# A two-layer hybrid encoder on one core: the left operands of the MLP's seven products are ordered behind the last bank read of the block before, squares go to ScalarE, derived low parts are made in two instructions

## The chip, the core and the metric

The kernel runs on one core of a Trainium2 chip. The metric is the device time of one execution in microseconds (us); lower is better. Times of before come from three plain runs and from one profiled execution, whose trace is what is read here.

## What is computed

The reference is a two-layer encoder trunk on 512 frames of width 1024 in float32. Layer 0 mixes tokens with a sparse attention, layer 1 with a latent attention, and each layer ends in a dense MLP with a squared ReLU. The change touches the two MLPs only:

```python
D_MODEL = 1024
SEQ = 512
DEPTH = 2
D_FF = 4 * D_MODEL

def squared_relu_mlp(h, w_up, w_down):
    a = jax.nn.relu(h @ w_up)
    return (a * a) @ w_down

    for i in range(DEPTH):
        h = rms_norm(x, attn_norm[i])
        ...
        h = rms_norm(x, mlp_norm[i])
        x = x + squared_relu_mlp(h, mlp_w_up[i], mlp_w_down[i])
    return rms_norm(x, final_norm)
```

## The kernel before, in words

**Three passes for one product.** Every float32 operand is split into a high part (rounded to the format that TensorE multiplies, `fp32r`) and a low part (what is left), and a product is three matmuls: high by high, high by low, low by high. For weights `Weights.convert` (from L112) does this: ScalarE casts the raw tile to `w_hi` (L143), GpSimd subtracts to get `w_lo` (L144), one instruction each for a tile of 128x1024. For activations in the MLP `part` (L1098 to L1104) does it on ScalarE (`lh`, L1102) and VectorE (`ll`, L1103), 128x512 each.

**The MLP in blocks.** `mlp` cuts the 4096 hidden columns into NB = 8 blocks of FB = 512. `up(b)` makes the hidden block `u`: four groups of 24 matmuls (8 slices of the width, three passes), 96 in all, each group into one PSUM bank; `square` then writes relu squared to `u` with a Relu on ScalarE (L1073) and a multiply on VectorE (L1074, which reads the bank again). For blocks 0 to 6 the second product is made by `left` and `down_quarters`: with `u` cut in two by two pieces and the block's weights too, seven products of half size replace eight (Winograd's form). `left` makes the seven left operands from the four pieces: four additions or subtractions on VectorE (L1114, L1115, L1117, L1119), in place in `u`, and seven `part`s. `Weights.quarters` makes the seven right operands from four quarter tiles `quad`: four subtractions on VectorE (L86), in place too, each followed by the conversion of its result. Because they are in place, a later subtraction waits until GpSimd has read the value before: the chain is `quad` subtraction, cast, low part, next subtraction. The seven weights of a block are called Q1 to Q7 below, the four weight tiles of its up half U1 to U4.

**Down.** `down_quarters` does seven steps of 12 matmuls, 84 in all. A step writes two PSUM banks, `pa` in the odd steps and `pb` in the even ones, and after its first six and its last six matmuls VectorE adds the bank to the residual `x` (L1141): 14 bank reads a block. Most steps go on accumulating in a bank that was read two steps earlier, so step s+2 waits for the bank reads of step s. The last block goes through `down`, which makes the full product.

**What sets the order.** The program is traced in the order `left(u of block b-1)`, `up(b)`, `down_quarters` of block b-1, and a scheduler with a timeline of its own orders the instructions of every engine at compile time. Each engine then runs its queue strictly in that order. `W.take` hands out converted weights; `WBUFS` = 5 pairs of `w_hi` and `w_lo` exist, so a tile is converted when TensorE has finished with the one five before it.

Of the kernel before, what the change touches and what calls it, by code (L numbers as in the profile page):

```python
# [11 lines left out]
F32 = mybir.dt.float32  # L12
F32R = mybir.dt.float32r
I32 = mybir.dt.int32
AF = mybir.ActivationFunctionType
OP = mybir.AluOpType
# [37 lines left out]
class Weights:  # L54
# [57 lines left out]
    def convert(self):  # L112
        i = len(self.done)
        if i >= len(self.items):
            return
        while len(self.raw) <= i:
            self.fetch()
        nc = self.nc
        src, a, n, engs, heads = self.items[i]
        raw = self.raw[i]  # L120
        if callable(src):
            heads = None
            if callable(raw):
                raw = raw()
        hi = self.parts.tile([P, a * n], F32R, name=f"w{i}_hi", tag="whi")
        lo = self.parts.tile([P, a * n], F32R, name=f"w{i}_lo", tag="wlo")
        views = [(raw, hi, lo)]
        if heads is not None:

            views = []  # L130
            for s in range(2):
                v = raw.rearrange("p (k h s d) -> p k h s d", k=a, h=heads, s=2)[:, :, :, s, :]
                o = [t.rearrange("p (k s h d) -> p k s h d", k=a, s=2, h=heads)[:, :, s, :, :] for t in (hi, lo)]
                views.append((v, *o))
        for v, h, l in views:
            if engs[0] == "p":
                shape = list(v.shape)
                one = self.ones
                while len(one.shape) < len(shape):
                    one = one[:, None]  # L140
                nc.gpsimd.tensor_tensor(h, v, one.to_broadcast(shape), op=OP.mult)
            else:
                nc.scalar.copy(h, v)  # L143
            (nc.gpsimd if engs[1] == "p" else nc.vector).tensor_sub(l, v, h.bitcast(F32))  # L144
        r = lambda t: t.rearrange("p (a n) -> p a n", a=a)
        self.done.append((r(hi), r(lo)))
        while len(self.raw) < min(len(self.done) + RAWS, len(self.items)):
            self.fetch()
# [50 lines left out]
def trunk(ctx: ExitStack, tc: tile.TileContext, x, positions, attn_norm, mlp_norm, a_w_in, a_w_out,  # L199
          b_w_in, b_q_norm, b_kv_norm, b_w_q_up, b_w_kv_up, b_w_out, mlp_w_up, mlp_w_down,  # L200
          final_norm, out):
    nc = tc.nc
# [6 lines left out]
    def bank(name, i):  # L209
        return psum.tile([P, 512], F32, name=name, tag=f"bank{i}")  # L210
# [9 lines left out]
    def mm3(ps, lh, ll, rh, rl, first, last):  # L220
        nc.tensor.matmul(ps, lh, rh, start=first, stop=False)  # L221
        nc.tensor.matmul(ps, lh, rl, start=False, stop=False)  # L222
        nc.tensor.matmul(ps, ll, rh, start=False, stop=last)  # L223
# [835 lines left out]
    def mlp(i, nm, follower):  # L1059
        with ExitStack() as sm:  # L1060
            mp = sm.enter_context(tc.tile_pool(name=f"mlp{i}", bufs=1, reuse_waits="tile"))
            W.quads = mp
            hi, lo = nm.hi, nm.lo
            up_b, dn_b = Banks(0, 1, 4, 5), Banks(6, 7, 2, 3)

            def up_mm(ps, ws, f, t0, t1):
                for k in range(KD):
                    wh, wl = ws[k // 4]
                    mm3(ps[:, t0:t1], wh[:, k % 4, f * P:(f + 1) * P], wl[:, k % 4, f * P:(f + 1) * P],
                        hi[:, k, t0:t1], lo[:, k, t0:t1], k == 0, k == KD - 1)  # L1070

            def square(ps, u, f):
                nc.scalar.activation(u[:, f, :], ps, AF.Relu)  # L1073
                nc.vector.scalar_tensor_tensor(u[:, f, :], ps, 0.0, u[:, f, :], op0=OP.max, op1=OP.mult)  # L1074

            def up(b):
                u = mp.tile([P, 4, S], F32, name="u", tag="u", bufs=2)
                if b == 0:

                    ws = W.take(2) + W.take(2, 2)  # L1080
                    pp = [up_b("up") for _ in range(4)]
                    for f in range(4):
                        up_mm(pp[f], ws[f // 2 * 2:][:2], f % 2, 0, S // 2)
                        if f % 2:
                            nm.turn(NT - 2 + f // 2)
                    for f in range(4):
                        up_mm(pp[f], ws[f // 2 * 2:][:2], f % 2, S // 2, S)
                        square(pp[f], u, f)
                    return u
                for c in range(FB // 256):  # L1090
                    ws = W.take(2)
                    for f in range(2):
                        ps = up_b("up")
                        up_mm(ps, ws, f, 0, S)
                        square(ps, u, 2 * c + f)
                return u

            def part(v):  # L1098

                lh = mp.tile([P, 2, S // 2], F32R, name="lh", tag="lh", bufs=8)  # L1100
                ll = mp.tile([P, 2, S // 2], F32R, name="ll", tag="ll", bufs=8)
                nc.scalar.copy(lh, v)  # L1102
                nc.vector.tensor_sub(ll, v, lh.bitcast(F32))  # L1103
                return lh, ll  # L1104

            def blocks(u):

                return [[u[:, 2 * k:2 * k + 2, i * 256:(i + 1) * 256] for k in range(2)] for i in range(2)]

            def left(u):  # L1110

                (a, b), (c, d) = blocks(u)
                l11, l22 = part(a), part(d)
                nc.vector.tensor_add(d, c, d)  # L1114
                nc.vector.tensor_sub(c, a, c)  # L1115
                s3 = part(c)
                nc.vector.tensor_sub(a, d, a)  # L1117
                s2, s1, l12 = part(a), part(d), part(b)
                nc.vector.tensor_sub(b, b, a)  # L1119
                return [l11, s3, s2, l22, s1, l12, part(b)]  # L1120

            def down_quarters(ops):

                pa, pb = [bank("dn", 6), bank("dn", 7)], [bank("dn", 2), bank("dn", 3)]

                steps = ((pa, True, (0, 0)), (pb, True, (1, 1)), (pa, False, (1, 0)), (pb, False, (1, 0)),
                         (pa, False, (1, 1)), (pb, True, (0, 0)), (pa, False, (0, 1)))  # L1130
                for (lh, ll), (pp, first, (i, j)) in zip(ops, steps):
                    wh, wl = W.take()[0]
                    cs = slice(j * 512, (j + 1) * 512)
                    for t in range(2):
                        ts = slice(t * P, (t + 1) * P)
                        for k in range(2):
                            for m, (l, r) in enumerate(((lh, wh), (lh, wl), (ll, wh))):
                                nc.tensor.matmul(pp[t], l[:, k, ts], r[:, k, :], start=first and k == 0 and m == 0,  # L1138
                                                 stop=k == 1 and m == 2, skip_group_check=True)
                        x = xt[2 * i + t]  # L1140
                        nc.vector.tensor_add(x[:, cs], pp[t], x[:, cs])  # L1141

            def down(u, after):
                ops = [[part(v) for v in row] for row in blocks(u)]
                ws = W.take(FB // P)
                for t in range(NT):
                    ts = slice(t % 2 * P, (t % 2 + 1) * P)
                    for c in range(2):
                        cs = slice(c * 512, (c + 1) * 512)
                        ps = dn_b("dn")  # L1150
                        for k in range(4):
                            wh, wl = ws[k]
                            lh, ll = ops[t // 2][k // 2]
                            mm3(ps, lh[:, k % 2, ts], ll[:, k % 2, ts], wh[:, 0, cs], wl[:, 0, cs], k == 0, k == 3)
                        nc.vector.tensor_add(xt[t][:, cs], ps, xt[t][:, cs])
                        after(t, c)

            prev = up(0)
            for b in range(1, NB):
                ops = left(prev)  # L1160
                prev = up(b)
                down_quarters(ops)
            nxt = follower()
            down(prev, nxt.follow)
        return nxt
# [10 lines left out]

    nm = mixer_a()
    nm = mlp(0, nm, lambda: Norm(attn_norm[1]))
    nm = mixer_b(nm)
    mlp(1, nm, Final)  # L1180


# [22 lines left out]
```

## Time and profile before

| What | us |
|---|---|
| median of three runs | 1190.31 (1190.16 to 1190.56) |
| profiled execution | 1191.61 |
| its span in the trace | 1189.8 |
| TensorE matmul busy | 1124.6 (95%) |
| VectorE busy | 876.9 (74%) |
| GpSimd busy | 650.0 (55%) |
| ScalarE busy | 561.8 (47%) |
| from the first matmul of `down_quarters` to the first of `down` in MLP 0 | 307.10 to 585.55 |
| the same in MLP 1 | 882.83 to 1161.21 |

In the rows of the profile PE is TensorE's matmul side, PEld its weight loads, DVE VectorE, ACT ScalarE, POOL GpSimd, SP SyncE. A row of the timeline has the start in us, the duration in us, engine, line, operation, output and inputs, shape and count, and in brackets how long the engine was idle before it and what ended that. A row of the chain of work that ended last has start, length and the work. A row of the groups has line, engine, operation, names, shapes and count, then busy us and the mean ns of one, then idle us before them and what ended it. Matmul durations are modelled with an overlap; the distance of their starts is the pace.

### The profile page before, as it was taken

How to read it: one execution, taken by the hardware profiler on the slowest of the kernel's cores; microseconds unless marked ns; L12 is line 12 of the kernel's file. 1: busy time of each engine (PE TensorE's matmuls, PEld its weight loads, DVE VectorE, ACT ScalarE, POOL GpSimd, SP SyncE). 2: the span in 40 equal slices, each digit the busy share in tenths (PEclk: the TensorE clock that was granted, in tenths of full speed). 3: DMA queues.
4: the chain of work that ended last, by engine and by line, in shares of the span. 5: the costliest groups of instructions: out<-in, count | busy, mean ns of one | idle time of the engine just before them, and what ended most of it. 6: DMA issues, size and time to landing. Idle time of an engine off the chain costs nothing.

```text
span 1189.8 us, 15782 instructions
## 1 busy us (share of the span) xinstructions
PE 1124.6 (95%) x5721; PEld 947.9 (80%) x5721; DVE 876.9 (74%) x1483; ACT 561.8 (47%) x1051; POOL 650.0 (55%) x397
## 2 busy tenths in 40 slices
PE   6899899999999999999999899899999999999997
PEld 5778778879777787787889788797987787787786
DVE  7599998765958757857567888985587857866864
ACT  5443786644433443433345666563443433434342
POOL 4457432553656755765603642735556665765771
PEclk9899899999999999999999999999999999999999
DMA  6422100251224323322312210111513322322401
GB/s 205 115 63 92 51 1 2 72 175 57 89 64 131 105 73 106 124 72 88 91 51 77 74 54 1 59 49 54 189 57 109 121 74 89 124 89 71 142 18 71
DMA packets 65605, 99.55 MB, mean 84 GB/s; under 512 B 3188, under 2 KB 41848, under 8 KB 65528
## 3 DMA queue, kind: packets, MB, share of 16 engines
q1 hardware_dynamic: 65528, 98.55, 25.8%
q8 instruction: 45, 0.74, 0.2%
q14 instruction: 32, 0.26, 0.1%
HBM read 96.44 MB, written 2.10 MB: 83 GB/s over the span
## 4 chain that ended last, share of the span: by engine, by line
PE 66%; DVE 28%; ACT 2%; issue 2%; DMA 1%; SPq 0%; POOL 0%; DVEq 0%; POOLq 0%; ACTq 0%
PE dn L1138 10%; PE up L223 10%; PE up L222 9%; PE up L221 9%; DVE ll L1103 5%; DVE x L1141 5%; PE s_ps L508 3%; PE o_ps L570 3%; PE wo_ps L221 2%; DVE u L1117 2%; DVE u L1115 2%; PE wo_ps L222 2%; PE wo_ps L223 2%; DVE u L1114 2%; PE pt_ps L527 2%
## 5 line engine op out<-in xcount | busy, mean ns | idle before, releaser
L144 POOL TENSOR_TENSOR w_lo<-w_raw,w_hi 128x1024 fp32r<-128x1024 f32 (+4 forms) x117 | 276.9, 2380 | 153.2 <-ACT w_hi L143 152.9
L144 POOL TENSOR_TENSOR w_lo<-quad,w_hi 128x1024 fp32r<-128x1024 f32 x98 | 247.2, 2541 | 138.6 <-ACT w_hi L143 138.6
L222 PE MATMUL up<-hT_lo,w_hi 128*128 128x512 f32 (+1 forms) x576 | 210.5, 366 | 0.0
L221 PE MATMUL up<-hT_hi,w_hi 128*128 128x512 f32 (+1 forms) x576 | 209.4, 366 | 0.1
L223 PE MATMUL up<-hT_hi,w_lo 128*128 128x512 f32 (+1 forms) x576 | 208.6, 366 | 0.0
L143 ACT CAST w_hi<-quad 128x1024 fp32r<-128x1024 f32 x98 | 101.7, 1051 | 164.1 <-DVE quad L86 135.1
L1138 PE MATMUL dn<-w_hi,lh 128*128 128x512 f32 x392 | 155.6, 397 | 20.9 <-DVE x L1141 20.1
L1141 DVE TENSOR_TENSOR x<-dn,x 128x512 f32<-128x512 f32 x196 | 130.4, 683 | 46.3 <-PE dn L1138 45.4
L1138 PE MATMUL dn<-w_hi,ll 128*128 128x512 f32 x392 | 152.8, 390 | 0.0
L1138 PE MATMUL dn<-w_lo,lh 128*128 128x512 f32 x392 | 152.7, 390 | 0.0
L143 ACT CAST w_hi<-w_raw 128x1024 fp32r<-128x1024 f32 (+6 forms) x108 | 109.1, 1018 | 74.9 <-PE dn L1138 23.3
L1103 DVE TENSOR_TENSOR ll<-u,lh 128x512 fp32r<-128x512 f32 x106 | 130.4, 1243 | 5.0 <-ACT lh L1102 4.8
L1102 ACT CAST lh<-u 128x512 fp32r<-128x512 f32 x106 | 63.8, 618 | 132.9 <-DVE u L1119 62.0
L86 DVE TENSOR_TENSOR quad<-quad 128x1024 f32<-128x1024 f32 x56 | 68.4, 1222 | 73.6 <-POOL w_lo L144 73.6
L222 PEld LDWEIGHTS up<-hT_lo,w_hi 128*128 128x128 f32 x576 | 108.6, 189 | 17.6 <-DVE hT_lo L422 0.2
L223 PEld LDWEIGHTS up<-hT_hi,w_lo 128*128 128x128 f32 x576 | 108.6, 189 | 17.5
L221 PEld LDWEIGHTS up<-hT_hi,w_hi 128*128 128x128 f32 x576 | 108.1, 189 | 17.9 <-ACT hT_hi L421 0.3
L1138 PEld LDWEIGHTS dn<-w_hi,lh 128*128 128x128 f32 x392 | 73.5, 188 | 47.0 <-DVE x L1141 31.9
L521 ACT ACTIVATE p<-p,m 128x128 f32<-128x128 f32 (+3 forms) x128 | 71.9, 563 | 32.4 <-DVE m L516 31.8
L1138 PEld LDWEIGHTS dn<-w_hi,ll 128*128 128x128 f32 x392 | 73.6, 188 | 15.5
L1138 PEld LDWEIGHTS dn<-w_lo,lh 128*128 128x128 f32 x392 | 73.6, 188 | 14.4
L1074 DVE SCALAR_TENSOR_TENSOR u<-up,u 128x512 f32<-128x512 f32 x64 | 44.0, 687 | 55.2 <-ACT u L1073 55.2
(223 smaller groups left out, 2313.1 us busy)
## 6 DMA issues: line engine op xcount, KB each, us to landing
w_raw<-in_mlp_w_up_dram SPq DMA_DIRECT2D x64, 512.0 KB, 3.6
quad<-in_mlp_w_down_dram SPq DMA_DIRECT2D x56, 512.0 KB, 3.6
w_raw<-in_a_w_in_dram SPq DMA_DIRECT2D x12, 512.0 KB, 3.6
w_raw<-in_a_w_out_dram SPq DMA_DIRECT2D x8, 512.0 KB, 3.2
w_raw<-in_mlp_w_down_dram SPq DMA_DIRECT2D x8, 512.0 KB, 3.6
w_raw<-in_b_w_out_dram SPq DMA_DIRECT2D x8, 512.0 KB, 3.7
x<-in_x_dram SPq DMA_DIRECT2D x4, 512.0 KB, 7.4
w_raw<-in_b_w_kv_up_dram SPq DMA_DIRECT2D x4, 512.0 KB, 3.8
```

The source lines that it names most:

```text
L86: self.nc.vector.tensor_sub(q[o], q[l], q[r])
L143: nc.scalar.copy(h, v)
L144: (nc.gpsimd if engs[1] == "p" else nc.vector).tensor_sub(l, v, h.bitcast(F32))
L221: nc.tensor.matmul(ps, lh, rh, start=first, stop=False)
L222: nc.tensor.matmul(ps, lh, rl, start=False, stop=False)
L223: nc.tensor.matmul(ps, ll, rh, start=False, stop=last)
L521: nc.scalar.activation(U["p"][:, :N], U["p"][:, :N], AF.Exp, bias=U["m"], scale=-1.0, accum_out=pair["sums"][:, c:c + 1])
L1074: nc.vector.scalar_tensor_tensor(u[:, f, :], ps, 0.0, u[:, f, :], op0=OP.max, op1=OP.mult)
L1102: nc.scalar.copy(lh, v)
L1103: nc.vector.tensor_sub(ll, v, lh.bitcast(F32))
L1138: nc.tensor.matmul(pp[t], l[:, k, ts], r[:, k, :], start=first and k == 0 and m == 0, stop=k == 1 and m == 2, skip_group_check=True)
L1141: nc.vector.tensor_add(x[:, cs], pp[t], x[:, cs])
```

## The change

Three edits. `down_quarters` returns its last bank read, and from the second block on `left` is traced with `issue_after` that instruction, which puts every VectorE instruction of `left` behind it in VectorE's queue (what `left` does on ScalarE is not bound by it). `square` multiplies on ScalarE, by a Square activation of `u` in place, in place of the VectorE multiply. `convert` makes the low part of a weight that comes from `quarters` (its `src` is a function) in two GpSimd instructions of 512 columns; other weights keep one of 1024.

```diff
-            (nc.gpsimd if engs[1] == "p" else nc.vector).tensor_sub(l, v, h.bitcast(F32))
+            if callable(src):
+
+                for c in range(0, a * n, 512):
+                    cs = slice(c, c + 512)
+                    nc.gpsimd.tensor_sub(l[:, cs], v[:, cs], h[:, cs].bitcast(F32))
+            else:
+                (nc.gpsimd if engs[1] == "p" else nc.vector).tensor_sub(l, v, h.bitcast(F32))
...
                 nc.scalar.activation(u[:, f, :], ps, AF.Relu)
-                nc.vector.scalar_tensor_tensor(u[:, f, :], ps, 0.0, u[:, f, :], op0=OP.max, op1=OP.mult)
+                nc.scalar.activation(u[:, f, :], u[:, f, :], AF.Square)
...
-                        nc.vector.tensor_add(x[:, cs], pp[t], x[:, cs])
+                        last = nc.vector.tensor_add(x[:, cs], pp[t], x[:, cs])
+                return last
...
             prev = up(0)
+            last = None
             for b in range(1, NB):
-                ops = left(prev)
+                with tc.issue_after(last.ins) if last is not None else ExitStack():
+                    ops = left(prev)
                 prev = up(b)
-                down_quarters(ops)
+                last = down_quarters(ops)
```

The changed file has other line numbers: L1141 becomes L1147, L1102 and L1103 become L1108 and L1109, L1114, L1115, L1117 and L1119 become L1120, L1121, L1123 and L1125, L1073 and L1074 become L1079 and L1080 (now on ScalarE), L144 becomes L148 for the two halves. Texts below use the numbers of before.

First place, VectorE in the second block of MLP 0. Before, its queue from the third bank read of a `down_quarters` on, in which `x_85` to `x_88` are the four tiles of the residual:

```order
L1141 TENSOR_TENSOR x_87<-dn,x_87 128x512
L1103 TENSOR_TENSOR ll<-u,lh 128x512
L1141 TENSOR_TENSOR x_88<-dn,x_88 128x512
L1114 TENSOR_TENSOR u<-u 128x2x256
L1141 TENSOR_TENSOR x_87<-dn,x_87 128x512
L1115 TENSOR_TENSOR u<-u 128x2x256
L1141 TENSOR_TENSOR x_88<-dn,x_88 128x512
L1117 TENSOR_TENSOR u<-u 128x2x256
```

Now, from behind the last bank read of a `down_quarters` to the first of the next:

```order
L1109 TENSOR_TENSOR ll<-u,lh 128x512 x2
L1120 TENSOR_TENSOR u<-u 128x2x256
L1121 TENSOR_TENSOR u<-u 128x2x256
L1123 TENSOR_TENSOR u<-u 128x2x256
L86 TENSOR_TENSOR quad<-quad 128x1024
L1109 TENSOR_TENSOR ll<-u,lh 128x512 x2
L86 TENSOR_TENSOR quad<-quad 128x1024
L1109 TENSOR_TENSOR ll<-u,lh 128x512 x2
L1125 TENSOR_TENSOR u<-u 128x2x256
L1109 TENSOR_TENSOR ll<-u,lh 128x512
L86 TENSOR_TENSOR quad<-quad 128x1024 x2
L1147 TENSOR_TENSOR x_85<-dn,x_85 128x512
```

All eleven instructions of `left` and the four `quad` subtractions now stand between two sets of 14 bank reads, and the 14 follow each other with nothing between them.

Second place, ScalarE over the same block. Before, the casts of the four up weights (`w_raw`) alternate with those of the left operands (`lh`):

```order
L143 CAST w_hi<-w_raw 128x1024
L1102 CAST lh<-u 128x512 x3
L143 CAST w_hi<-w_raw 128x1024
L1102 CAST lh<-u 128x512
L143 CAST w_hi<-w_raw 128x1024
L1102 CAST lh<-u 128x512
L143 CAST w_hi<-w_raw 128x1024
L143 CAST w_hi<-quad 128x1024
L1073 ACTIVATE u<-up 128x512
L143 CAST w_hi<-quad 128x1024
L1073 ACTIVATE u<-up 128x512
```

Now:

```order
L143 CAST w_hi<-w_raw 128x1024 x4
L143 CAST w_hi<-quad 128x1024
L1108 CAST lh<-u 128x512 x4
L1079 ACTIVATE u<-up 128x512
L1080 ACTIVATE u<-u 128x512
L143 CAST w_hi<-quad 128x1024
L1079 ACTIVATE u<-up 128x512
L1108 CAST lh<-u 128x512
L1080 ACTIVATE u<-u 128x512
L1108 CAST lh<-u 128x512
L143 CAST w_hi<-quad 128x1024
```

The four up casts and the first `quad` cast now stand ahead of the left operands' casts, and a Square follows each Relu. On GpSimd the order is unchanged, each `w_lo<-quad` row of 1024 columns being two rows of 512; on TensorE three matmuls of the next `up` move by some places within the last steps of `down_quarters`; SyncE's queue is the same.

## The prediction

> **What bounds the kernel now.** I read the page first, for the engines and for the chain that ended last.
>
> ```profile
> span 1189.8 us, 15782 instructions
> PE 1124.6 (95%) x5721; PEld 947.9 (80%) x5721; DVE 876.9 (74%) x1483; ACT 561.8 (47%) x1051; POOL 650.0 (55%) x397
> ...
> PE 66%; DVE 28%; ACT 2%; issue 2%; DMA 1%; SPq 0%; POOL 0%; DVEq 0%; POOLq 0%; ACTq 0%
> ```
>
> TensorE is the bound, but 28% of the chain lies on VectorE, so somewhere TensorE waits for it. Second, the chain in order of time over one middle block of MLP 0.
>
> ```profile
> 437.87 4.09 PE dn L1138 x18
> ...
> 444.04 2.13 DVE u L1114
> 446.17 0.60 DVE x L1141
> 446.77 2.21 DVE u L1115
> ...
> 449.58 2.22 DVE u L1117
> ...
> 454.20 2.75 DVE ll L1103
> 456.95 0.61 DVE x L1141
> ...
> 457.61 3.02 PE dn L1138 x12
> ```
>
> The chain leaves TensorE soon after the seven products begin, runs along VectorE's queue through the subtractions and low parts of `left`, and comes back by a bank read (L1141): the reads are late because `left` stands between them. Third, the timeline of TensorE at that place and at the starts of `dn`, the first matmul of a `down_quarters` (rows of several windows).
>
> ```profile
> 307.10 0.39 PE L1138 MATMUL dn<-w_hi,lh 128*128 128x512 f32 x1
> ...
> 328.81 0.50 PE L1138 MATMUL dn<-w_hi,lh 128*128 128x512 f32 x1 [1.46 <-DVE x L1141]
> ...
> 351.84 0.39 PE L1138 MATMUL dn<-w_hi,lh 128*128 128x512 f32 x1
> ...
> 455.76 0.39 PE L1138 MATMUL dn<-w_hi,ll 128*128 128x512 f32 x1
> 457.61 0.50 PE L1138 MATMUL dn<-w_hi,lh 128*128 128x512 f32 x1 [1.46 <-DVE x L1141]
> ...
> 480.64 0.39 PE L1138 MATMUL dn<-w_hi,lh 128*128 128x512 f32 x1
> ...
> 566.51 0.39 PE L1138 MATMUL dn<-w_hi,lh 128*128 128x512 f32 x1
> ...
> 882.83 0.39 PE L1138 MATMUL dn<-w_hi,lh 128*128 128x512 f32 x1
> ...
> 927.57 0.39 PE L1138 MATMUL dn<-w_hi,lh 128*128 128x512 f32 x1
> ...
> 1142.17 0.39 PE L1138 MATMUL dn<-w_hi,lh 128*128 128x512 f32 x1
> ```
>
> How fast a `down_quarters` can be is shown by the last of MLP 0, for which no `left` is queued between the bank reads (the chain again):
>
> ```profile
> 566.67 19.04 PE dn L1138 x84
> ```
>
> 84 matmuls in 19.04 us are 0.2267 us each. From one start of `dn` to the next there are 84 + 96 = 180 matmuls, 40.80 us at that pace. Measured: 351.84 - 307.10 = 44.74, then (566.51 - 351.84) / 5 = 42.93 in each of five blocks; in MLP 1 44.74 and (1142.17 - 927.57) / 5 = 42.92. So TensorE loses 3.94 + 5 x 2.13 + 3.94 + 5 x 2.12 = 29.1 us in twelve blocks. This is all that the change can win there.
>
> **Why `left` is slow under the products.** The groups by shape:
>
> ```profile
> L144 POOL TENSOR_TENSOR w_lo<-quad,w_hi 128x1024 fp32r<-128x1024 f32 x98 | 247.2, 2541 | 138.6 <-ACT w_hi L143 138.6
> L144 POOL TENSOR_TENSOR w_lo<-w_raw,w_hi 128x512 fp32r<-128x512 f32 x6 | 7.7, 1304 | 0.0
> L1103 DVE TENSOR_TENSOR ll<-u,lh 128x512 fp32r<-128x512 f32 x106 | 130.4, 1243 | 5.0 <-ACT lh L1102 4.8
> L1141 DVE TENSOR_TENSOR x<-dn,x 128x512 f32<-128x512 f32 x196 | 130.4, 683 | 46.3 <-PE dn L1138 45.4
> L86 DVE TENSOR_TENSOR quad<-quad 128x1024 f32<-128x1024 f32 x56 | 68.4, 1222 | 73.6 <-POOL w_lo L144 73.6
> L1074 DVE SCALAR_TENSOR_TENSOR u<-up,u 128x512 f32<-128x512 f32 x64 | 44.0, 687 | 55.2 <-ACT u L1073 55.2
> L1115 DVE TENSOR_TENSOR u<-u 128x512 f32<-128x512 f32 x14 | 28.8, 2059 | 0.0
> L1119 DVE TENSOR_TENSOR u<-u 128x512 f32<-128x512 f32 x14 | 9.7, 690 | 0.4
> L1102 ACT CAST lh<-u 128x512 fp32r<-128x512 f32 x106 | 63.8, 618 | 132.9 <-DVE u L1119 62.0
> L1073 ACT ACTIVATE u<-up 128x512 f32<-128x512 f32 x64 | 37.9, 593 | 38.5 <-PE up L223 38.4
> ```
>
> L1115 and L1119 are the same operation on the same shape, at 2.06 and 0.69 us. What differs is GpSimd beside them:
>
> ```profile
> 448.39 2.86 POOL L144 TENSOR_TENSOR w_lo<-w_raw,w_hi 128x1024 fp32r<-128x1024 f32 x1
> 454.00 5.19 POOL L144 TENSOR_TENSOR w_lo<-w_raw,w_hi 128x1024 fp32r<-128x1024 f32 x2 [2.76 <-ACT w_hi L143]
> ...
> 462.22 2.41 POOL L144 TENSOR_TENSOR w_lo<-w_raw,w_hi 128x1024 fp32r<-128x1024 f32 x1 [3.02 <-ACT w_hi L143]
> ```
>
> L1117 began at 449.58 inside the first of these and ended 451.80, 0.55 after it (448.39 + 2.86 = 451.25); the `ll` at 454.20 ended at 456.95, 0.35 after half of the pair at 454.00. So a VectorE instruction with both inputs in SBUF waits for the GpSimd instruction that has begun, then takes 0.6; the bank reads, with one input in PSUM, take 0.68 whatever GpSimd does. [...]
>
> **The change part by part.**
>
> Order of `left`. It removes from the 14 bank reads everything between them, so each can go at about its bank's end, as in the stretch of 19.04 us. Gain 29.1 us, if nothing else comes late. What it moves: seven `ll`, four subtractions of `left` and four `quad` subtractions now stand in the stretch of the next `up`, 91 matmuls or 20.6 us, ahead of the next bank reads. I set 0 at the end of the last `dn` matmul. The last bank read, 0.68 long, is done at about 1. Two `ll` and L1114 share the time with Q1's low part, whose cast waits for the end of `dn`: L1114 done at about 5.2, L1115 and L1117 at 6.4. First `quad` 6.4 to 7.6, `ll` of the third and fourth operand to 8.8 (their casts ran meanwhile on ScalarE), second `quad` to 10.0. Then the in-place chain, its steps by these rows:
>
> ```profile
> 470.15 1.05 ACT L143 CAST w_hi<-quad 128x1024 fp32r<-128x1024 f32 x1 [4.58 <-DVE quad L86]
> ...
> 471.28 2.40 POOL L144 TENSOR_TENSOR w_lo<-quad,w_hi 128x1024 fp32r<-128x1024 f32 x1 [4.29 <-ACT w_hi L143]
> ...
> 473.71 1.23 DVE L86 TENSOR_TENSOR quad<-quad 128x1024 f32<-128x1024 f32 x1 [1.29 <-POOL w_lo L144]
> ...
> 478.53 1.23 DVE L86 TENSOR_TENSOR quad<-quad 128x1024 f32<-128x1024 f32 x1 [1.29 <-POOL w_lo L144]
> ```
>
> Cast 10.2 to 11.2, Q2's low part in two halves of 1.30 with one `ll` let in between, to 14.6; the rest of `left` is done by then; third `quad` to 16.0; cast to 17.2, Q3's low part to 19.9, fourth `quad` to 21.1. The next `dn` starts at 20.6, and its first six matmuls end at 22.0, so VectorE is free a microsecond early. TensorE would be held only if the first bank read ended after step 3 begins, 20.6 + 24 x 0.2267 = 26.0, that is if the fourth `quad` ended after 25.1: 4 us of room. Weights, at the same pace of one low part per 2.6 and 2.4 us: Q4 ready at about 25 (wanted at step 4, 28.8), Q7 at 32.5 (step 7, 38.1), U1's low part at 35 (its first matmul in the queue, 37.9). Before, the fourth `quad` began at 478.53, 2.1 us ahead of the start of `dn` at 480.64; by this schedule it begins 0.7 ahead, so the chain has moved by 1.4 us of its room.
>
> In the first block of each MLP `left` isn't bound, but the 3.94 us lost there are of the same kind: the wait at 328.81 is for a bank read, behind the `left` of the second block, and that one is bound.
>
> Squares. 64 VectorE multiplies of 0.69 go, four a block; none is on the chain, so their going is worth 0. ScalarE gets 64 squares. No row has this one; the nearest are the Relu at 593 ns and the cast of the same shape from SBUF at 618. I take 0.62, since input and output are in SBUF, 2.5 us a block on an engine that is busy 17.2 of 42.93:
>
> ```profile
> 437.87:480.80 42.93, 41.39 (x181) 33.62 (x181) 30.82 (x33) 17.20 (x24) 27.98 (x11) 1.00 0.31 98
> ```
>
> (The columns are the stretch, its length, and busy us of TensorE, its weight loads, VectorE, ScalarE and GpSimd.) What waits behind them are the second `quad` cast and two casts of `left`, at most 1.2 us of the 4 us room. ScalarE's queue keeps the two table loads that it had. Cost 0, within 1 us either way at the first and last block of an MLP, where `u` is awaited.
>
> Halves. 98 GpSimd instructions become 196. Two of 1.30 are 2.61, against 2.41 undisturbed: +0.2 us each, 1.4 a block on GpSimd, not on the path. They halve what VectorE waits. [...]
>
> Sum: 1191.61 - 29.1 = 1162.5 for a profiled execution. That one stood 1.3 above the median, so 1161.2 for the median.
>
> **The rivals.**
>
> 1. GpSimd's round becomes the bound. By the schedule above the last low part of a round ends at about 41 to 43 with the period at 40.80: Q1 cannot begin early, and Q2, Q3 and Q4 each wait for VectorE. If `left` and GpSimd stop each other more than I count, say by 2 us a block, the round takes 42 to 43, the lateness adds up by 1.5 a block, the 3 to 4 us of room last two or three blocks, and the other three pay 1.5 to 2: 2 x 3 x 1.75 = 10 us lost again, 1172. For it: the round is within 2 us of the period, and low parts do get longer beside VectorE (2.86 at 448.39 against 2.41 at 462.22). [...] Against: today's collisions lengthen GpSimd's 11 instructions only from 26.5 (11 x 2.41) to 27.98, and at a period of 40.80 it would still be idle for 11 us.
>
> 2. Slower: the waits of `left` stay as long as they are under the products. Place: the fourth `quad` and behind it the bank reads. If all eleven instructions of `left` cost 2.06, they are 22.7 us, with the four `quad`s 4.9, and the last ends at 1 + 27.6 = 28.6, 3.5 past the limit of 25.1. TensorE then loses 3.5 a block, against 2.13 now: 10 x 1.4 - 2 x 0.4 = 13 more, 1203. It decides from 27.2 on, 6 us later than I expect. Against: GpSimd is idle for good parts of this stretch (3.02 and 4.29 us ahead of the low parts at 462.22 and 471.28), and the halves cut each wait.
>
> 3. It doesn't do what it says: the loss is elsewhere, and 1190 stays. Against: the chain names the bank reads in the block shown, and the five middle blocks of either MLP have the same mean period to 0.01 us.
>
> **How the numbers follow.** Forecast 0.72, rival 1 0.16, rival 2 0.07, rival 3 0.05. The gain needs no price that the trace lacks, only that about 15 us of VectorE work end within 24. The range goes from 1159 (2 us for the bounds of the squares and of the pace) to 1172, which takes in rival 1 up to its price. A measurement of this kernel can tell 0.2%, 2.4 us, from no change. Faster by more: forecast, rival 1 and a little of rival 3, 0.89; within: 0.04; slower: 0.07.
>
> **What would show it.** Right: starts of `dn` 40.8 apart, no wait of a `dn` matmul for L1141 within a block, the chain almost all on TensorE there, L1115 well under 2.06, a square near 0.62, halves near 1.30. The steps are wrong if the periods lie above 41.3 with waits for weights (rival 1), if the fourth `quad` ends more than 4.5 us after the start of `dn` (rival 2), or if the periods are 40.8 and the time has not fallen, which would mean time lost outside the MLPs.

## The result and the profile after

| Kernel | Median of its runs, us | Ratio to before (95%) |
|---|---|---|
| before | 1190.43 (1190.16 to 1190.56) | |
| changed | 1162.22 (1161.57 to 1163.72) | 0.9765 [0.9748, 0.9782] |
| changed, a second time, beside a before of 1191.59 | 1162.62 | 0.9759 [0.9745, 0.9772] |

The ratios here and below leave out one execution of the kernel with the order alone, which took 1249.79 us at a granted clock of 0.85.

The profiled execution took 1162.26 us, 29.35 less than that of before. First the page: the span, the engines, and the shares of the chain that ended last.

```profile
span 1160.5 us, 15969 instructions
PE 1116.6 (96%) x5721; PEld 949.8 (82%) x5721; DVE 782.3 (67%) x1419; ACT 604.3 (52%) x1115; POOL 666.0 (57%) x495
...
PE 79%; DVE 12%; issue 3%; ACT 3%; POOL 1%; DMA 1%; SPq 0%; DVEq 0%; POOLq 0%; ACTq 0%
```

TensorE's share of the chain rose from 66% to 79%, VectorE's fell from 28% to 12%. The timeline of TensorE at starts of `dn` in the changed kernel:

```profile
306.27 0.39 PE L1144 MATMUL dn<-w_hi,lh 128*128 128x512 f32 x1
...
347.07 0.39 PE L1144 MATMUL dn<-w_hi,lh 128*128 128x512 f32 x1
...
551.07 0.39 PE L1144 MATMUL dn<-w_hi,lh 128*128 128x512 f32 x1
...
868.03 0.39 PE L1144 MATMUL dn<-w_hi,lh 128*128 128x512 f32 x1
...
1112.83 0.39 PE L1144 MATMUL dn<-w_hi,lh 128*128 128x512 f32 x1
```

347.07 - 306.27 = 40.80, (551.07 - 306.27) / 6 = 40.80, (1112.83 - 868.03) / 6 = 40.80. From the first start to the last, MLP 0 takes 244.80 in place of 259.41 and MLP 1 244.80 in place of 259.34: 29.15 of the 29.35 us. The remainder outside these stretches is small because two changes cancel: the first `dn` starts 0.83 us earlier, and MLP 0's last block takes 0.7 us longer. The groups by shape of the changed kernel:

```profile
L148 POOL TENSOR_TENSOR w_lo<-quad,w_hi 128x512 fp32r<-128x512 f32 x196 | 275.0, 1433 | 162.9 <-ACT w_hi L143 160.3 <-PE up L229 2.4
L1147 DVE TENSOR_TENSOR x<-dn,x 128x512 f32<-128x512 f32 x196 | 135.0, 691 | 138.4 <-PE dn L1144 138.4
L1109 DVE TENSOR_TENSOR ll<-u,lh 128x512 fp32r<-128x512 f32 x106 | 99.4, 968 | 40.8 <-ACT lh L1108 40.8
L1080 ACT ACTIVATE u<-u 128x512 f32<-128x512 f32 x64 | 40.4, 632 | 1.7
L1120 DVE TENSOR_TENSOR u<-u 128x512 f32<-128x512 f32 x14 | 23.3, 1664 | 0.5
L1121 DVE TENSOR_TENSOR u<-u 128x512 f32<-128x512 f32 x14 | 12.6, 901 | 0.5
```

L1120 and L1121 (L1114 and L1115 of before) fell from 2003 and 2059 ns to 1664 and 901. The bank read still takes 0.69, but it now waits 138.4 us for `dn` where it waited 46.3: at the bank reads VectorE waits for TensorE, no longer the other way round. A square takes 632 ns, a half 1433.

The timeline between two sets of bank reads in a middle block of MLP 0; the next `dn` starts at 469.47. First VectorE, then GpSimd, then two rows of ScalarE.

```profile
449.04 0.69 DVE L1147 TENSOR_TENSOR x<-dn,x 128x512 f32<-128x512 f32 x1 [0.67 <-PE dn L1144]
449.65 4.28 DVE L1109 TENSOR_TENSOR ll<-u,lh 128x512 fp32r<-128x512 f32 x2
453.97 1.67 DVE L1120 TENSOR_TENSOR u<-u 128x512 f32<-128x512 f32 x1
...
457.00 1.22 DVE L86 TENSOR_TENSOR quad<-quad 128x1024 f32<-128x1024 f32 x1
...
470.34 1.22 DVE L86 TENSOR_TENSOR quad<-quad 128x1024 f32<-128x1024 f32 x1 [3.74 <-POOL w_lo L148]
471.49 0.68 DVE L1147 TENSOR_TENSOR x<-dn,x 128x512 f32<-128x512 f32 x1
```

```profile
449.29 2.40 POOL L150 TENSOR_TENSOR w_lo<-w_raw,w_hi 128x1024 fp32r<-128x1024 f32 x1 [0.47 <-ACT w_hi L143]
451.65 3.44 POOL L148 TENSOR_TENSOR w_lo<-quad,w_hi 128x512 fp32r<-128x512 f32 x2
461.86 3.48 POOL L148 TENSOR_TENSOR w_lo<-quad,w_hi 128x512 fp32r<-128x512 f32 x2 [6.77 <-ACT w_hi L143]
467.77 2.54 POOL L148 TENSOR_TENSOR w_lo<-quad,w_hi 128x512 fp32r<-128x512 f32 x2 [2.42 <-ACT w_hi L143]
```

```profile
448.16 1.05 ACT L143 CAST w_hi<-w_raw 128x1024 fp32r<-128x1024 f32 x1 [4.59 <-DMA w_raw<-in_mlp_w_up_dram]
449.17 1.05 ACT L143 CAST w_hi<-quad 128x1024 fp32r<-128x1024 f32 x1
```

The schedule of the prediction is there, in its order, but 1.6 to 1.8 us later from the end of the first subtraction on. Its zero is 469.47 - 20.63 = 448.84, so the first `quad` began at 8.2 (forecast 6.4) and the fourth ended at 471.56, or 22.7 (forecast 21.1, limit 25.1). The cast of U4 waited 4.59 us for its DMA, so U4's low part fell at 449.29, onto the first two `ll` of `left`, with Q1's halves behind it. The prediction had put Q1's low part alone beside them.

### The profile page after: what moved, and what is told of

Read it like the earlier page. It is cut to its first block, busy times and chain, and to the rows that moved or that the text cites. A ratio compares the mean times of both kernels' runs of the same rounds, so it can differ in the third digit from the quotient of the medians.

```text
span 1160.5 us, 15969 instructions
## 1 busy us (share of the span) xinstructions
PE 1116.6 (96%) x5721; PEld 949.8 (82%) x5721; DVE 782.3 (67%) x1419; ACT 604.3 (52%) x1115; POOL 666.0 (57%) x495
## 4 chain that ended last, share of the span: by engine, by line
PE 79%; DVE 12%; issue 3%; ACT 3%; POOL 1%; DMA 1%; SPq 0%; DVEq 0%; POOLq 0%; ACTq 0%
PE dn L1144 22%; PE up L227 10%; PE up L228 10%; PE up L229 10%; PE s_ps L514 3%; PE o_ps L576 3%; PE wo_ps L227 2%; PE wo_ps L228 2%; PE wo_ps L229 2%; PE pt_ps L533 2%; DVE bias L779 2%; DVE m L777 2%; PE dn L228 1%; PE dn L229 1%; PE dn L227 1%
## 5 line engine op out<-in xcount | busy, mean ns | idle before, releaser
L148 POOL TENSOR_TENSOR w_lo<-quad,w_hi 128x512 fp32r<-128x512 f32 x196 | 275.0, 1433 | 162.9 <-ACT w_hi L143 160.3
L150 POOL TENSOR_TENSOR w_lo<-w_raw,w_hi 128x1024 fp32r<-128x1024 f32 (+4 forms) x117 | 265.0, 2284 | 89.0 <-ACT w_hi L143 88.6
L1147 DVE TENSOR_TENSOR x<-dn,x 128x512 f32<-128x512 f32 x196 | 135.0, 691 | 138.4 <-PE dn L1144 138.4
L1144 PE MATMUL dn<-w_hi,lh 128*128 128x512 f32 x392 | 152.6, 389 | 0.2 <-ACT w_hi L143 0.2
L1109 DVE TENSOR_TENSOR ll<-u,lh 128x512 fp32r<-128x512 f32 x106 | 99.4, 968 | 40.8 <-ACT lh L1108 40.8
L1108 ACT CAST lh<-u 128x512 fp32r<-128x512 f32 x106 | 62.9, 621 | 76.3 <-DVE u L1121 67.9
L619 POOL TENSOR_TENSOR oh<-o,ones 128x512 fp32r<-128x512 f32 x16 | 16.7, 1044 | 95.3 <-DVE o L613 65.3
```

What stands on the lines that cost most here:

```text
L148: nc.gpsimd.tensor_sub(l[:, cs], v[:, cs], h[:, cs].bitcast(F32))
L1147: last = nc.vector.tensor_add(x[:, cs], pp[t], x[:, cs])
```

## The experiments

The theory (A where an expectation uses a letter) is the prediction's: the bank reads were late because `left` stood between them and each of its instructions waited for GpSimd's whole low part (2.06 us in place of 0.69); the order edit takes that away, and squares and halves are worth nothing beside it. Against it stand two rivals: that the gain comes from shorter waits or from VectorE's lighter load, that is from halves or squares; and that GpSimd's round is near its bound and lateness adds up. An expectation that means another rival says so. Ratios are to a kernel before timed in the same rounds, 1191.59 to 1191.66 us.

**The order alone**, the first edit of three:

```diff
-                        nc.vector.tensor_add(x[:, cs], pp[t], x[:, cs])
+                        last = nc.vector.tensor_add(x[:, cs], pp[t], x[:, cs])
+                return last
...
+            last = None
...
-                ops = left(prev)
+                with tc.issue_after(last.ins) if last is not None else ExitStack():
+                    ops = left(prev)
...
-                down_quarters(ops)
+                last = down_quarters(ops)
```

> The kernel before with the first edit alone: left is queued behind the last bank read, the squares stay on VectorE and the low parts of the seven weights stay whole (1024 columns). Theory A (the loss was bank reads standing behind left in VectorE's queue, and 20.6 us of up matmuls hide left): the starts of dn are 40.80 apart as in the changed kernel, 1162 to 1164 us. Theory B (the loss was the length of the waits of left for whole GpSimd instructions, and the halves are what made the order pay): the chain of quad subtractions and low parts ends over 2.4 us later than in the changed kernel, whose fourth quad ended 22.7 us after the end of dn against a limit of 25.1, TensorE waits again, 1167 us or more.

Measured 1166.17, 0.9783 [0.9768, 0.9797]. All periods are 40.8 but one, the last of MLP 0, which is 41.1. So the order alone removes nearly all of the loss that the prediction counted. It gives some back in the last block of each MLP, where waits are new; in the timeline of TensorE:

```profile
560.74 0.50 PE L1138 MATMUL dn<-w_hi,lh 128*128 128x512 f32 x1 [0.23 <-DVE x L1141]
...
563.64 0.47 PE L1138 MATMUL dn<-w_hi,lh 128*128 128x512 f32 x1 [1.24 <-ACT w_hi L143]
```

From the last start of `dn` to the first matmul behind the MLP it is 38.87 us, in before 36.63 and in the changed kernel 37.37. From the last start of `dn` in MLP 1 to the end of the span it is 50.05, in before and in the changed kernel 47.7. Timed again:

> Order alone again, beside the changed kernel. Its trace had periods of 40.80 in eleven of twelve blocks and 41.1 in one, so theory A gives the time of the changed kernel within 2 us; theory B, by which the halves are worth something with the order, at least 2 us more than the changed kernel in these rounds.

Measured 1165.97, 0.9788 [0.9775, 0.9802]: 3.35 us more than the changed kernel in the same rounds. The expectation gave this to theory B, so halves or squares are worth something beside the order, though not in the periods.

**The halves alone**, the third edit (`if callable(src):` and the loop over 512 columns), all else as before:

> The kernel before with the third edit alone: low parts of the seven weights in two instructions of 512 columns, left among the bank reads as before, squares on VectorE. Theory A in its narrow form (only the order matters): about 1190, at best 1185. Theory B: L1114, L1115, L1117 and the long ll waited 1.4 to 2.1 us each for a whole GpSimd instruction; with halves they wait about half, 3 us less in all, more than the 1.9 us by which the bank reads came late, so the period falls to 40.8 to 41.5 and the time to 1163 to 1171. If so either edit alone does it, and the two are not additive.

Measured 1180.2, 0.9902 [0.9887, 0.9917]; periods 42.46 to 42.56 in MLP 0. VectorE and GpSimd in its timeline:

```profile
439.86 1.18 DVE L1120 TENSOR_TENSOR u<-u 128x512 f32<-128x512 f32 x1
...
444.97 4.00 DVE L1109 TENSOR_TENSOR ll<-u,lh 128x512 fp32r<-128x512 f32 x2
...
449.50 2.28 DVE L1109 TENSOR_TENSOR ll<-u,lh 128x512 fp32r<-128x512 f32 x1
```

```profile
433.73 11.87 POOL L148 TENSOR_TENSOR w_lo<-quad,w_hi 128x512 fp32r<-128x512 f32 x8 [2.47 <-ACT w_hi L143]
445.56 8.46 POOL L150 TENSOR_TENSOR w_lo<-w_raw,w_hi 128x1024 fp32r<-128x1024 f32 x3
```

The subtractions beside halves fell from 2.2 to 1.18 us each, as the wait for a whole instruction says. But the low parts of the up weights are still whole, GpSimd reaches them without a pause, and three `ll` that now fall beside them take 4.00 and 2.28. The wait moved down the queue; 1.7 of the 2.13 us a block stay lost. So the time met neither expected range (1185 to 1190, 1163 to 1171).

**All low parts in halves, no order.** If the length of GpSimd's instruction is the cause, halving those of the up weights too should free the reads without any reordering. Against the third edit, only the condition differs:

```diff
-            if callable(src):
+            if heads is None and engs[1] == "p" and a * n == 1024:
```

> The kernel before (left among the bank reads, squares on VectorE) with every low part of 1024 columns made in two halves, those of the up weights and of the attention weights too. With halves for the seven weights alone L1114 to L1117 fell to 1.1 us each, but two ll beside a whole low part of an up weight took 4.00 and one 2.28, and the period was 42.48. If the wait for a begun GpSimd instruction is all of it, these fall to about 2.4 and 1.2, 2.7 us less than the 1.55 that TensorE still waited: period 40.8 to 41.1, 1162 to 1167. If left among the reads costs by its place, the period stays above 42.

Measured 1166.08, 0.9787 [0.9774, 0.9801]; periods 40.8, 41.0, then 41.6 to 41.7. No `dn` matmul waits for a bank read any more; of TensorE's waits in the blocks one row is left:

```profile
PE up L229 <- POOL w_lo L148: 4.3, 8, 0.6
```

and the timelines of TensorE and of GpSimd show where it is:

```profile
446.19 0.50 PE L229 MATMUL up<-hT_hi,w_lo 128*128 128x512 f32 x1 [0.55 <-POOL w_lo L148]
```

```profile
432.11 12.34 POOL L148 TENSOR_TENSOR w_lo<-quad,w_hi 128x512 fp32r<-128x512 f32 x8 [2.50 <-ACT w_hi L143]
444.41 12.47 POOL L148 TENSOR_TENSOR w_lo<-w_raw,w_hi 128x512 fp32r<-128x512 f32 x8
```

With the instructions of `left` still between the reads, the low parts of the left operands fell about as expected (2.4 and 1.2): the two `ll` from 4.00 to 2.89 us, the one from 2.28 to 1.16. So the reads come free by shorter waits alone. But eight weights now take GpSimd 24.8 us, 3.1 each where an undisturbed pair of halves takes 2.53 (at 456.85), and TensorE waits at 446.19 for the first of the up weights. This is rival 1 of the prediction, in a kernel that lacks the order: GpSimd's queue becomes the bound, at 0.85 us a block. The periods missed the expected 40.8 to 41.1; the time is inside its range with the help of 1.7 us outside the MLPs (see the end of the next section). The length of GpSimd's instruction did decide here: beside whole low parts the subtractions of `left` took 2.2 us, beside halves 1.18, and over all 106 the mean `ll` fell from 1.43 us with the halves alone to 1.00.

**The squares alone**, the second edit.

```diff
-                nc.vector.scalar_tensor_tensor(u[:, f, :], ps, 0.0, u[:, f, :], op0=OP.max, op1=OP.mult)
+                nc.scalar.activation(u[:, f, :], u[:, f, :], AF.Square)
```

> The kernel before with the second edit alone: the squares on ScalarE, left among the bank reads, low parts whole. Both theories: the four multiplies of 0.69 us that a block loses on VectorE stood in front of one bank read or in idle time, so within 2 us of 1190. A rival by which VectorE's total load is what counts: VectorE loses 2.7 of 30.8 us a block, and the 2.13 us of waits go, 1165.

Measured 1174.51, 0.9854 [0.9839, 0.9869], periods 42.6 in the first block and 41.75 to 41.80 behind it: half of the loss won by an edit that I had put at 0. In its timeline:

```profile
401.80 0.68 DVE L1141 TENSOR_TENSOR x<-dn,x 128x512 f32<-128x512 f32 x1
402.40 0.68 DVE L1117 TENSOR_TENSOR u<-u 128x512 f32<-128x512 f32 x1
```

```profile
396.11 5.21 POOL L144 TENSOR_TENSOR w_lo<-quad,w_hi 128x1024 fp32r<-128x1024 f32 x2 [0.60 <-ACT w_hi L143]
403.56 10.83 POOL L144 TENSOR_TENSOR w_lo<-w_raw,w_hi 128x1024 fp32r<-128x1024 f32 x4 [2.23 <-ACT w_hi L143]
```

GpSimd pauses from 401.3 to 403.56, L1117 and an `ll` fall into the pause and take 0.68. The multiplies no longer stand between the reads either, and the scheduler has chosen another order. To see whether ScalarE's load alone does it, the multiplies stay and ScalarE gets a second Relu of the same size:

```diff
                 nc.scalar.activation(u[:, f, :], ps, AF.Relu)
+                nc.scalar.activation(u[:, f, :], u[:, f, :], AF.Relu)
```

> The kernel before with a second Relu of u in place on ScalarE, ahead of VectorE's multiply; it changes no value. ScalarE has the load that squares on ScalarE gave it, VectorE keeps its four multiplies. Squares alone had brought the period from 42.93 to 41.78. If that came from GpSimd's low parts starting later, behind ScalarE's casts, and so leaving L1117 alone (0.68 us in place of 2.2), the period here is near 41.8 too and the time near 1175. If it came from VectorE's load, it stays at 42.9 and 1190.

Measured 1187.4, 0.9967 [0.9956, 0.9978]; periods 43.71 and 43.88 in the first blocks, 42.84 to 42.94 in the others. So ScalarE's load doesn't do it. It is the going of the multiplies from VectorE's queue, or the order that followed; these two weren't separated.

**Two edits of three.** Order and halves, and halves and squares without the order:

> Order and halves, squares on VectorE. Theory A: periods of 40.80 again, and whatever is left over lies in the last block of each MLP; 1161 to 1167. If the squares on ScalarE are what the halves need (four more VectorE instructions ahead of the fourth quad), the fourth quad ends over 25.1 us after the end of dn and the periods are longer.

Measured 1162.88, 0.9760 [0.9745, 0.9774]; periods 40.8.

> Halves and squares with left among the bank reads: the change without its order. Halves alone took 10 us off, squares alone 17. Theory A: part of the waits stays, since left still stands between the reads, period 41.0 to 41.8, 1164 to 1175. Theory B: nothing is left to win by the order, 40.8 and 1162.

Measured 1167.29, 0.9797 [0.9782, 0.9812]: 40.80 for the first three periods of each MLP, then 41.7 with a bank read waited for. Order and squares, low parts whole, beside the changed kernel once more:

> Order and squares, low parts whole. Theory A: like the changed kernel within 2 us, since the fourth quad ends no later than 25.1 us after the end of dn with whole low parts too; theory B: longer by over 2 us.

> The changed kernel itself once more, beside the next three on one chip, so that order alone (1166.17 us, 0.978 of before) can be told from all three edits (1162.22, 0.977). Both theories: 0.976 to 0.978 of before, periods of 40.80.

Measured 1160.88, 0.9742 [0.9729, 0.9756], and 1162.62, 0.9759 [0.9745, 0.9772], for the changed kernel. All periods are 40.80 in both. With order and squares, low parts whole, the block shown for the changed kernel reads, in the timelines of VectorE and GpSimd:

```profile
450.66 3.51 DVE L1103 TENSOR_TENSOR ll<-u,lh 128x512 fp32r<-128x512 f32 x2
454.20 0.69 DVE L1114 TENSOR_TENSOR u<-u 128x512 f32<-128x512 f32 x1
...
469.29 1.23 DVE L86 TENSOR_TENSOR quad<-quad 128x1024 f32<-128x1024 f32 x1 [3.59 <-POOL w_lo L144]
```

```profile
461.12 2.90 POOL L144 TENSOR_TENSOR w_lo<-quad,w_hi 128x1024 fp32r<-128x1024 f32 x1 [7.50 <-ACT w_hi L143]
466.86 2.40 POOL L144 TENSOR_TENSOR w_lo<-quad,w_hi 128x1024 fp32r<-128x1024 f32 x1 [2.85 <-ACT w_hi L143]
```

The low parts on the chain take 2.90 and 2.40 whole, 3.48 and 2.54 in halves: in this block, with the squares on ScalarE, the halves lengthen the chain by 0.7 us. The next table has when the fourth `quad` ends, in us after the start of `dn`, block by block of MLP 0 (one execution each):

| Kernel | 1 | 2 | 3 | 4 | 5 | 6 | 7 |
|---|---|---|---|---|---|---|---|
| before | 0.91 | -0.88 | -0.88 | -0.88 | -0.88 | -0.88 | -0.88 |
| changed | -0.54 | 0.08 | 1.30 | 1.77 | 2.09 | 2.12 | 2.16 |
| order alone | 0.36 | 0.90 | 1.99 | 2.11 | 2.54 | 2.96 | 2.82 |
| order and halves | -0.38 | 0.01 | 0.42 | 0.24 | 0.81 | 1.33 | 2.22 |
| order and squares | -1.16 | 0.03 | 1.36 | 0.56 | 0.04 | 0.03 | 0.03 |

In the changed kernel the chain gets later from block to block, as rival 1 says, and uses half of its room; with order and squares it does not. In MLP 1 the changed kernel reaches only 0.93, and its second run 1.84 and 1.78 in the two MLPs, so the drift differs between executions. Whole low parts by themselves don't end it: the order alone has them and drifts most (2.96, and 2.99 in MLP 1). Beside the order alone (1165.97) the halves win 3 us and the squares 5; with the squares there, the halves win nothing more (1160.88 without, 1162.62 with). Order and squares is the best median of the study, though its interval overlaps the changed kernel's.

**Where the limit lies.** Extra VectorE instructions ahead of the fourth `quad` of the changed kernel, four or two (each leaves the value as it is):

```diff
                 for o, l, r in subs:
+                    for _ in range(2 if (o, l, r) == (1, 2, 1) else 0):
+                        self.nc.vector.tensor_tensor(q[o], q[o], q[o], op=OP.max)
                     self.nc.vector.tensor_sub(q[o], q[l], q[r])
```

> The changed kernel with four more VectorE instructions of 1.22 us ahead of the fourth quad subtraction (the larger of a tile and itself, in place, which changes no value), so that the fourth weight comes 4.9 us later. Theory A with its limit: in the changed kernel the fourth quad ends 22.7 us after the end of dn, so it now ends at 27.6; its cast and low part take 3.8 more, 31.4, and step 4 of the products wants it at 28.8: TensorE waits 2.6 us a block in twelve blocks, 1162 + 31 = 1193, between 1185 and 1200. If the chain had room to spare (no wait until about 33 us), the time stays at 1162.

Measured 1267.98, 1.0639 [1.0621, 1.0657], periods 48.2 to 50.6 from the second block of each MLP on (40.8 in the first, where a bank read stands ahead of the fourth `quad`). The scheduler moved the first two `quad`s too and put bank reads between the extra instructions, so the fourth `quad` ended 12.4 to 14.7 us after the start of `dn` and TensorE waited for Q4. The edit was not the delay that I meant, and the limit can't be read from it. With two:

> The changed kernel with two more VectorE instructions of 1.22 us ahead of the fourth quad. In the changed kernel the fourth quad ends some 2 us after the start of dn, with a limit of 4.5; it now ends 2.4 later, at 4.5, just at the limit: waits of 0 to 1 us a block, 1162 to 1175. If the limit lies lower than worked out, or the chain grows by more than the added 2.4 as it did with four, over 1175.

Measured 1194.09, 1.0025 [1.0013, 1.0037]; the execution profiled took 1198.23, the longest of its ten. VectorE of one block, in which `dn` started at 389.33:

```profile
392.97 2.48 DVE L87 TENSOR_TENSOR quad<-quad 128x1024 f32<-128x1024 f32 x2 [3.74 <-POOL w_lo L150]
395.49 1.22 DVE L88 TENSOR_TENSOR quad<-quad 128x1024 f32<-128x1024 f32 x1
396.64 2.48 DVE L1149 TENSOR_TENSOR x<-dn,x 128x512 f32<-128x512 f32 x4
```

Behind the two extra ones (L87) the fourth `quad` ended at 396.71, 7.4 after the start, and four bank reads that should have been done follow in a row. Over the other blocks of MLP 0:

| End of the fourth `quad` after the start of `dn`, us | Period, us | Over 40.80 |
|---|---|---|
| 1.98 | 40.80 | 0 |
| 5.26 | 41.48 | 0.68 |
| 5.88 | 42.10 | 1.30 |
| 7.45 | 43.69 | 2.89 |
| 7.52 | 43.73 | 2.93 |

Every late row gives a limit of 4.56 to 4.59 (5.26 - 0.68, 7.52 - 2.93); the prediction had 4.5. Delays beyond the limit cost one for one in these rows; the block shown, and two of MLP 1, cost 1.5 to 1.6 more, for which the last section has the reason. And the two instructions, 2.48 us together, moved the end by 2.5 in the first block but by 5.2 in the second. There the first two `ll` took 4.38 us in place of 1.29, and the scheduler had put two more `ll` ahead of the second `quad`. So lateness adds up here by more than the edit, but adding up and changed order were not separated.

## Why the prediction was right

**The loss and its place.** 29.1 us were forecast, 29.15 came, in the stretch from the first `dn` to the last and with all twelve periods at 40.80. The pace of 84 matmuls in 19.04 us held for a whole block. That the whole time came out as well was in part luck: the prediction gave everything to the order, but the order alone stands at 1166, since the last block of each MLP then gets 2.2 to 2.4 us longer, and it took squares or halves, put at 0, to win that back. The forecast of 1162.5 for a profiled execution stands against 1162.26; the median is 1 us above the 1161.2, since this profile stood at the median and not 1.3 above it.

**The cause.** It has two parts, and each was tested. That the reads were late because `left` stood between them: the order alone takes `left` away, and all but one of the periods are 40.8. That an instruction of `left` "waits for the GpSimd instruction that has begun": shortening GpSimd's instructions and leaving `left` where it was frees the reads too (2.2 to 1.18 us for a subtraction; with all low parts in halves no `dn` matmul waits for a read). So the order is one of two cures that suffice for the reads, and the rival of the experiments, that halves and squares are worth something by themselves, holds too: 11.5 us for the halves alone, 17.1 for the squares alone. The gains do not add (with the 25.5 of the order they would be 54), because each shortens the same 29 us.

**The schedule.** Its order was right, its times 1.6 to 1.8 us early: the step that failed is "Two `ll` and L1114 share the time with Q1's low part", which left out U4's low part. The room of 4 us paid for it, so this error did not reach the time. The limit itself was right to 0.1 us.

**Squares.** 0.62 was estimated, 0.632 measured. That "none is on the chain, so their going is worth 0" is right beside order and halves (1162.88 without squares, 1162.2 to 1162.6 with), and wrong otherwise: beside the order alone the edit won 5 us (1165.97 to 1160.88), by itself 17.

**Halves.** 1.30 each was estimated from undisturbed rows, 1.433 is the mean: pairs beside VectorE take 3.44 and 3.48, an undisturbed one 2.54. That the halves are "not on the path" failed: the pairs of Q2 and Q3 (461.86 and 467.77) lie on the chain of the `quad`s. It costs nothing in the periods only because of the room.

**Rival 1** exists as a mechanism and not at its price: the chain drifts by 2.7 us in MLP 0 (from -0.54 to 2.16), levels off there, and has 2.4 us left to the limit of 4.57. Among the kernels with the order the drift is gone only where the low parts are whole and the squares are on ScalarE; which wait hands the lateness on is not shown. It decides where the room is less (the kernel with two extra instructions) or where all low parts are in halves. **Rival 2** needed the fourth `quad` 4.6 us late; it was 2.2 at most. **Rival 3** fell with the periods.

**Not foreseen.** In the last block of MLP 0 one matmul waits 0.17 us for a cast, and the changed kernel is 0.7 us longer there than before.

```profile
559.56 0.47 PE L1144 MATMUL dn<-w_hi,lh 128*128 128x512 f32 x1 [0.17 <-ACT w_hi L143]
```

This matmul starts 0.56 after the one ahead of it in place of 0.23. It is the small form of the wait that costs the order alone most of its 2.2 us in MLP 0. The seven products there lose 0.46 us in all in the changed kernel; the rest is lost in `down`. With order and halves the products lose nothing and `down` loses 0.7, at this wait:

```profile
573.96 0.50 PE L228 MATMUL dn<-w_lo,lh 128*128 128x512 f32 x1 [0.36 <-POOL w_lo L150]
```

With order and squares nothing is lost in either. So halves or squares each relieve the wait of the order alone, and the halves bring a smaller one in `down`; why the conversions come late there was not tried. Open too: the stretch from the end of MLP 0 to the start of the second MLP, which no edit but the halving of all low parts touches, took 233.1 us before and after but 231.4 to 231.6 with the order alone, the squares alone, the second Relu and all halves. So differences of 1 to 2 us between these kernels can't be put down to the MLPs.

## What to carry to other kernels

Look first at what stands in a queue between the instructions that the bound engine waits for; moving it behind them can win the whole wait, where shortening it wins a part and passes the wait on to the next long neighbour (here 25.5 us by the order alone, 11.5 by the halves alone). Work out the latest time at which the moved chain may end and how late it is from block to block, since lateness that adds up may fit seven blocks and not seventy. Edits that shorten the same wait do not add, so test each alone and in pairs: here halves or squares were enough beside the order, and the two together won no more than the squares.

## What the runs showed of the hardware

After some waits of about 3 us TensorE was granted a lower clock, 0.60 in the case shown here. In the kernel with two extra instructions TensorE waited from 394.8 to 397.47 in the block shown, and then:

```profile
398.14 0.63 PE L1146 MATMUL dn<-w_hi,ll 128*128 128x512 f32 x1
398.57 0.63 PE L1146 MATMUL dn<-w_hi,lh 128*128 128x512 f32 x1
399.00 0.63 PE L1146 MATMUL dn<-w_lo,lh 128*128 128x512 f32 x1
```

The starts are 0.43 apart in place of 0.227, until 401.1. The row of the windows for this stretch has the granted clock after the busy times:

```profile
397.00:401.00 4.00, 3.53 (x9) 2.85 (x10) 2.81 (x5) 4.00 (x5) 3.07 (x3) 0.60 0.02 6
```

It is 0.60, and the period is 45.22, 1.6 us more than the limit of 4.57 explains. Between starts the gap here was 2.92 us. In the same execution seven gaps were between 2.9 and 3.4 us: 2.92, 2.93, 3.04 and 3.36 were followed by matmuls at 0.43, and 2.99, 3.05 and 3.33 cost nothing. Behind the gap of 3.04 four matmuls still ran at the full pace before the slow ones began. In the kernel with four extra instructions all twelve gaps of 5.0 to 7.5 us were followed by the slow pace (behind the one of 5.07 the granted clock was 0.58 from 410 to 414), and none of the gaps up to 2.1. The slow stretches lasted 3.1 to 3.4 us in three of the four cases and 6.1 in the other.

So gaps of nearly one length went both ways: the pace fell behind one of 2.92 us and held behind one of 3.33. What length of idle time is enough is not shown.

A wait of VectorE's making near 3 us so cost 1.5 to 1.6 us more than its own length in three periods, and nothing more in others.
